# The triangular block inverses of the gated delta rule: their products and subtractions issued on VectorE instead of GpSimd

## The chip, the cores and the metric

The kernel runs on one core of one Trainium2 chip. The metric is the device time of one execution in microseconds; the time quoted for a kernel is the median of its runs. Beside it stands one profiled execution, whose trace gives the start and length of every instruction on TensorE (PE, with its weight loads as PEld), VectorE (DVE), ScalarE (ACT), GpSimd (POOL) and the DMA queues.

## The reference

The program is a two-layer encoder trunk on 512 tokens of 1024 channels in fp32. Layer 0 mixes with attention, layer 1 with a gated DeltaNet of 8 heads of 128 channels; each layer has a half-step SwiGLU feed-forward block before and after its mixer. The change lies in the DeltaNet. There the tokens are cut into chunks, and each chunk of each head needs the inverse of a unit lower triangular matrix:

```
    l_mat = jnp.where(strict, jnp.einsum('bhncd,bhnsd->bhncs', kb, k) * decay, 0.0)
    t_mat = lax.linalg.triangular_solve(l_mat + eye, jnp.broadcast_to(eye, l_mat.shape),
                                        left_side=True, lower=True, unit_diagonal=True)
    u = jnp.einsum('bhncs,bhnsd->bhncd', t_mat, vb)
    def step(state, inp):
        v_new = un - jnp.einsum('bhcd,bhde->bhce', wn, state)
        o = jnp.einsum('bhcd,bhde->bhce', qd, state) + jnp.einsum('bhcs,bhse->bhce', aqk, v_new)
        state = state * cd[..., None, None] + jnp.einsum('bhcd,bhce->bhde', kd, v_new)
```

## The kernel before

All large products are fp32 matmuls made of three products of split operands (`mm3`, lines 179 to 183): weights arrive by SP's DMA queue in panels (`panel`, line 163), ACT rounds a panel to `wh` (line 174) and DVE makes the rest `wl` (line 175). Three panels are held split at a time.

The DeltaNet layer (`odd_mixer`, line 711) takes the eight heads as four pairs, p = 0 to 3. Its projections, gates and output products are one stream, the filler, on TensorE; their results are evicted from two PSUM banks (`mm`) by DVE, as `cx` (line 924, with a depthwise convolution `cy`, lines 927 to 931, behind it) or as `gy` (line 773). Between the filler's steps stand the steps of the delta rule. For one pair of heads they are:

- prep (`gdn_keys`, line 945): the chunk matrices `iu` (line 980) and `du` (line 988) for 128 tokens at a time;
- base (`gdn_base`, line 1016): the inverses of the 32x32 diagonal blocks, 32 blocks to a pair. ACT's DMA queue writes `iu` to DRAM (`iud`, line 1023) and reads the blocks back as `lb`, one block's row per partition (line 1029). Then 31 steps j follow, each a product into `tmp` (line 1035) and a subtraction from `rr` (line 1038) over at most 76 elements per partition, each of these 62 operations needing the one ahead of it. The finished `rr` goes to DRAM by four DMAs on ACT's queue (`rd`, line 1041), and two more bring it back as `r`, one for each head (line 1044);
- scan (`gdn_head`, line 1047): DVE turns `r` into `t` (line 1053); TensorE starts with the products of `t` and `iu` (line 1063, in the trace the rows `pb<-t,iu` with 32*32), doubles the inverses to 64 and 128 rows (lines 1066 to 1083), and then passes over four blocks of 128 tokens, where each block's products wait for DVE's `vb` (lines 1094, 1099) and `state` (lines 1107, 1110). At the end `rs` (line 160, on POOL) scales the output `on` (line 1131), which TensorE turns back (line 784).

The order in which TensorE takes filler and steps is written out: `blend` (line 64) deals the steps by the due times in the table `PLAN`, and a helper keeps the matmuls in that order (line 95). For the other engines a scheduler works out the order of their queues when the program is built, from the order of the program and its own estimate of durations. Each engine takes its queue in order, and an instruction that waits holds all behind it; ACT's DMA issues stand in ACT's queue too. There is one `lb`, one `rr` and one `tmp`, so that a base of one pair begins after the base of the pair ahead.

Of the kernel before, what the change touches and what calls it, by code (L numbers as in the profile page):

```python
# [13 lines left out]
ALU = mybir.AluOpType  # L14
# [87 lines left out]
class Trunk:  # L102
# [913 lines left out]
    def gdn_base(self, pool, G, Ks):  # L1016


        nc = self.nc
        n = BASE  # L1020
        iud = self.dram.tile([2 * HPITCH], F32, tag="iud", name="iud", bufs=2)
        for j, K in enumerate(Ks):
            nc.scalar.dma_start(self.rows_of(iud, j), K["iu"].rearrange("p (t s) -> p t s", s=P))
        lb = pool.tile([P, n, n], F32, tag="lb", name="lb", bufs=1)
        rr = pool.tile([P, n // 4, n], F32, tag="rr", name="rr", bufs=1)
        tmp = pool.tile([P, 9 * n], F32, tag="tmp", name="tmp", bufs=1)
        quarters = [slice(q * 2 * NBLK, (q + 1) * 2 * NBLK) for q in range(4)]
        for s in quarters:
            nc.scalar.dma_start(lb[s], self.blocks_of(iud))
        nc.scalar.copy(out=rr, in_=G["eye"])  # L1030
        for j in range(n - 1):
            m, k = n - 1 - j, j // 4 + 1
            sh = [P, k, m]
            p = tmp[:, :k * m].rearrange("p (a b) -> p a b", b=m)
            nc.gpsimd.tensor_tensor(p, rr[:, :k, j:j + 1].broadcast_to(sh),  # L1035
                                    lb[:, j, j + 1:].rearrange("p (o m) -> p o m", o=1)
                                    .broadcast_to(sh), op=ALU.mult)
            nc.gpsimd.tensor_tensor(rr[:, :k, j + 1:], rr[:, :k, j + 1:], p, op=ALU.subtract)  # L1038
            yield
        for q, s in enumerate(quarters):  # L1040
            nc.scalar.dma_start(self.blocks_of(G["rd"], q, 4), rr[s])
        for j, K in enumerate(Ks):
            K["r"] = pool.tile([P, T], F32, tag="r", name="r", bufs=3)
            nc.scalar.dma_start(K["r"].rearrange("p (t s) -> p t s", s=P), self.rows_of(G["rd"], j))
        yield
# [156 lines left out]
```

## Time and profile before

| what | value |
|---|---|
| median of 3 runs | 2044.92 us (2044.28 to 2045.09) |
| the profiled execution: its own time, its span | 2044.75 us, 2042.9 us |
| TensorE busy | 2011.8 us, 98% of the span |
| DVE, ACT, POOL busy | 1086.6, 747.5, 129.6 us |
| mean granted TensorE clock over the span | 0.994 of full speed |

Busy time of TensorE holds matmuls whose ends are modelled and overlap, so its share says only where it stood idle. In rows of the time line a line in brackets at the end tells how long the engine stood idle before the row and what ended that. A granted clock of 1.00 is TensorE's 2.4 GHz level, and a stretch below it holds time at the 1.2 GHz level.

### The profile page before, as it was taken

Reading aid. Unit: us, or ns where it says so; the run is one execution under the profiler, and the core shown is the slowest. Engines: PE = TensorE matmul, PEld = TensorE weight load, DVE = VectorE, ACT = ScalarE, POOL = GpSimd, SP = SyncE. Lnnn points to the kernel's source line nnn. Section 1 sums busy time; section 2 is a strip of 40 time slices with the busy share of each in tenths; the row PEclk is TensorE's granted clock in tenths of the full one; section 3 lists DMA queues with packets and bytes.
Section 4 is the critical chain, followed back from the end, with each engine's and each line's share of the span. In section 5 each row is a group of like instructions: output and inputs, shape, how many; then the busy total and the mean of one; then the engine's idle time right before and its main releaser. Section 6 shows DMA issues by size and latency. Waiting matters only on the chain.

```text
span 2042.9 us, 24836 instructions
## 1 busy us (share of the span) xinstructions
PE 2011.8 (98%) x9786; PEld 1669.5 (82%) x9786; DVE 1086.6 (53%) x1752; ACT 747.5 (37%) x1359; POOL 129.6 (6%) x294
## 2 busy tenths in 40 slices
PE   8999999999999999999999999998999999999998
PEld 7888888878888888888888888877877788888887
DVE  6442444587676443444544344477677675443543
ACT  5231233454663322323332123354455453322222
POOL 0000000000000000000000000005432400000000
PEclk9999999999999999999999999999999999999999
DMA  4332323222123233232332232334322333323232
GB/s 156 97 99 93 103 93 95 93 70 66 52 75 112 93 94 102 93 102 95 93 98 98 93 103 93 95 114 110 85 75 88 80 99 98 103 83 103 93 98 78
DMA packets 189866, 192.24 MB, mean 94 GB/s; under 512 B 28546, under 2 KB 165044, under 8 KB 189748
## 3 DMA queue, kind: packets, MB, share of 16 engines
q1 hardware_dynamic: 158916, 182.62, 28.5%
q10 hardware_dynamic: 30832, 8.02, 1.7%
q8 instruction: 77, 1.26, 0.3%
q14 instruction: 41, 0.34, 0.1%
HBM read 185.35 MB, written 5.26 MB: 93 GB/s over the span
## 4 chain that ended last, share of the span: by engine, by line
PE 89%; POOL 5%; DMA 2%; DVE 1%; issue 1%; ACT 1%; ACTq 0%; SPq 0%; POOLq 0%
PE mm L181 10%; PE mm L183 10%; PE mm L182 10%; PE pa L181 8%; PE pa L183 8%; PE pa L182 8%; PE pb L181 8%; PE pb L182 8%; PE pb L183 8%; PE mm L96 4%; POOL rr L1038 2%; POOL tmp L1035 2%; PE pb L96 1%; DMA lb<-iud 1%; DMA iud<-iu 1%
## 5 line engine op out<-in xcount | busy, mean ns | idle before, releaser
L175 DVE TENSOR_TENSOR wl<-raw,wh 128x1024 fp32r<-128x1024 f32 (+1 forms) x348 | 413.6, 1189 | 564.5 <-ACT wh L174 563.7
L174 ACT CAST wh<-raw 128x1024 fp32r<-128x1024 f32 (+1 forms) x348 | 355.4, 1021 | 707.5 <-PE pb L182 279.9
L181 PE MATMUL mm<-xnh,wh 128*128 128x512 f32 (+1 forms) x816 | 317.3, 390 | 0.6 <-ACT wh L174 0.6
L183 PE MATMUL mm<-xnh,wl 128*128 128x512 f32 (+1 forms) x816 | 317.8, 390 | 0.0
L182 PE MATMUL mm<-xnl,wh 128*128 128x512 f32 (+1 forms) x816 | 316.8, 389 | 0.0
L181 PEld LDWEIGHTS mm<-xnh,wh 128*128 128x128 f32 x816 | 153.9, 189 | 32.8 <-ACT wh L174 1.2
L183 PEld LDWEIGHTS mm<-xnh,wl 128*128 128x128 f32 x816 | 154.0, 189 | 32.0 <-issue 1.6
L182 PEld LDWEIGHTS mm<-xnl,wh 128*128 128x128 f32 x816 | 154.0, 189 | 30.6 <-issue 0.7
L181 PE MATMUL pa<-xnh,wh 128*128 128x512 f32 x400 | 156.3, 391 | 0.0
L183 PE MATMUL pa<-xnh,wl 128*128 128x512 f32 x400 | 155.8, 390 | 0.0
L183 PE MATMUL pb<-xnh,wl 128*128 128x512 f32 x400 | 155.8, 389 | 0.0
L181 PE MATMUL pb<-xnh,wh 128*128 128x512 f32 x400 | 155.8, 389 | 0.0
L182 PE MATMUL pb<-xnl,wh 128*128 128x512 f32 x400 | 155.8, 389 | 0.0
L182 PE MATMUL pa<-xnl,wh 128*128 128x512 f32 x400 | 155.8, 389 | 0.0
L226 ACT CAST hid<-hd 128x512 fp32r<-128x512 f32 x88 | 54.6, 620 | 209.1 <-DVE hd L398 209.1
L96 PE MATMUL mm<-xnh,wh 128*128 128x512 f32 x256 | 109.7, 428 | 11.5 <-DVE cx L924 11.5
L392 DVE TENSOR_TENSOR gr<-mm,rb 128x512 f32<-128x512 f32 x80 | 55.3, 691 | 94.7 <-PE mm L183 94.5
L182 PE MATMUL pb<-hid,wh 128*128 128x512 f32 x264 | 102.8, 389 | 0.0
L183 PE MATMUL pb<-hid,wl 128*128 128x512 f32 x264 | 102.8, 389 | 0.0
L181 PE MATMUL pa<-hid,wh 128*128 128x512 f32 x264 | 102.8, 389 | 0.0
L183 PE MATMUL pa<-hid,wl 128*128 128x512 f32 x264 | 102.8, 389 | 0.0
L181 PE MATMUL pb<-hid,wh 128*128 128x512 f32 x264 | 102.8, 389 | 0.0
(307 smaller groups left out, 3372.7 us busy)
## 6 DMA issues: line engine op xcount, KB each, us to landing
raw<-in_ffn_w_gate_dram SPq DMA_DIRECT2D x88, 512.0 KB, 3.6
raw<-in_ffn_w_up_dram SPq DMA_DIRECT2D x88, 512.0 KB, 3.5
raw<-in_ffn_w_down_dram SPq DMA_DIRECT2D x88, 512.0 KB, 3.6
raw<-in_gdn_w_in_dram SPq DMA_DIRECT2D x32, 512.0 KB, 3.9
raw<-in_att_w_in_dram SPq DMA_DIRECT2D x24, 512.0 KB, 3.5
raw<-in_gdn_w_out_dram SPq DMA_DIRECT2D x16, 256.0 KB, 2.7
xr<-in_x_dram SPq DMA_DIRECT2D x4, 512.0 KB, 5.4
raw<-in_att_w_out_dram SPq DMA_DIRECT2D x4, 512.0 KB, 3.3
```

What stands on the lines that cost most here:

```text
L96: return self.tc.keep_in_program_order(self.engine.matmul(*args, **kw))
L174: nc.scalar.copy(out=h[:, :n], in_=raw[:, :n])
L175: nc.vector.tensor_tensor(l[:, :n], raw[:, :n], h[:, :n].bitcast(F32), op=ALU.subtract)
L181: self.te.matmul(out, lhsT=lh, rhs=rh, start=start, stop=False)
L182: self.te.matmul(out, lhsT=lh, rhs=rl, start=False, stop=False)
L183: self.te.matmul(out, lhsT=ll, rhs=rh, start=False, stop=stop)
L226: nc.scalar.copy(out=h, in_=src)
L392: nc.vector.tensor_tensor(gr, g[j], self.rb, op=ALU.mult)
L1035: nc.gpsimd.tensor_tensor(p, rr[:, :k, j:j + 1].broadcast_to(sh), lb[:, j, j + 1:].rearrange("p (o m) -> p o m", o=1) .broadcast_to(sh), o ...
L1038: nc.gpsimd.tensor_tensor(rr[:, :k, j + 1:], rr[:, :k, j + 1:], p, op=ALU.subtract)
```

## The change

Both operations of each of the 31 steps are issued on DVE instead of POOL, for all four pairs: 248 instructions. Nothing else in the source differs.

```
             p = tmp[:, :k * m].rearrange("p (a b) -> p a b", b=m)
-            nc.gpsimd.tensor_tensor(p, rr[:, :k, j:j + 1].broadcast_to(sh),
+            nc.vector.tensor_tensor(p, rr[:, :k, j:j + 1].broadcast_to(sh),
                                     lb[:, j, j + 1:].rearrange("p (o m) -> p o m", o=1)
                                     .broadcast_to(sh), op=ALU.mult)
-            nc.gpsimd.tensor_tensor(rr[:, :k, j + 1:], rr[:, :k, j + 1:], p, op=ALU.subtract)
+            nc.vector.tensor_tensor(rr[:, :k, j + 1:], rr[:, :k, j + 1:], p, op=ALU.subtract)
             yield
```

The scheduler lays out the queues of DVE and ACT anew; those of TensorE and SP stay as they are. Three places follow.

On DVE, at the end of the base of pair 0 (the rows from the change's queue set against that of before; + is new). Ahead of this piece, behind the first of two `gy` of line 773, stand the other 35 operations of the base's last 41, one behind the other.

```order
+L1035 TENSOR_TENSOR tmp<-rr,lb 128x24
+L1038 TENSOR_TENSOR rr<-rr,tmp 128x8x3
+L1035 TENSOR_TENSOR tmp<-rr,lb 128x16
+L1038 TENSOR_TENSOR rr<-rr,tmp 128x8x2
+L1035 TENSOR_TENSOR tmp<-rr,lb 128x8
+L1038 TENSOR_TENSOR rr<-rr,tmp 128x8
+L1053 STREAM_TRANSPOSE t<-r 128x512 x2
 L1066 TENSOR_SCALAR pp<-pb 32x128 x4
 L773 TENSOR_TENSOR gy<-mm,rb 128x512
```

The base now ends on DVE directly ahead of the transposes that read its result back, with no other work between. The first 21 operations of this base stand further ahead, singly between other DVE rows.

On ACT, around the DMAs that carry `rr` of pair 0 out and back (lines 1041 and 1044), this was the queue before:

```order
655 L174 CAST wh<-raw 128x1024
656 L932 ACTIVATE c<-cy 128x512
657 L1041 DMA rd<-rr 32x8x32 x4
658 L927 ACTIVATE cy<-cx,conv 128x512
659 L932 ACTIVATE c<-cy 128x512
660 L174 CAST wh<-raw 128x1024
661 L1044 DMA r<-rd 128x4x128 x2
```

So the issue stood ahead of the `cy` that begins the next convolution. In the change the same DMAs of pair 0 stand here on ACT:

```order
666 L970 ACTIVATE kdec<-pa,kd 128x128 x8
667 L774 ACTIVATE gy<-gy 128x512
668 L1041 DMA rd<-rr 32x8x32 x4
669 L1044 DMA r<-rd 128x4x128 x2
670 L1030 COPY rr<-eye 128x256
671 L174 CAST wh<-raw 128x1024
672 L774 ACTIVATE gy<-gy 128x512
```

The issue has moved behind that `cy` and behind the next pair's `kdec` and the first `gy`, and no other work stands between its two halves.

On DVE, where the base of pair 2 begins while pair 1 is in its scan (the change's queue).

```order
1173 L1099 COPY vb<-pb 128x128 x2
1174 L988 SCALAR_TENSOR_TENSOR du_10766<-pb,br,du_10766 128x128 x4
1175 L988 SCALAR_TENSOR_TENSOR du_10804<-pb,br,du_10804 128x128 x4
1176 L1110 COPY state<-pb 128x128 x2
1177 L1035 TENSOR_TENSOR tmp<-rr,lb 128x31
1178 L1038 TENSOR_TENSOR rr<-rr,tmp 128x31
1179 L175 TENSOR_TENSOR wl<-raw,wh 128x512
1180 L1035 TENSOR_TENSOR tmp<-rr,lb 128x30
1181 L785 SCALAR_TENSOR_TENSOR gy<-pa,head,gy 128x512
1182 L1038 TENSOR_TENSOR rr<-rr,tmp 128x30
```

The first product, which waits for the DMAs of line 1029, now stands in the queue of the engine that serves the scan; before, `wl` followed directly on `state`. On POOL the 248 rows are gone, and the operations of line 160 stand behind nothing.

## Rows read from the trace of the kernel before

**Rows 1.** The profile's page, part 1: busy us (share of the span) xinstructions.

```profile
PE 2011.8 (98%) x9786; PEld 1669.5 (82%) x9786; DVE 1086.6 (53%) x1752; ACT 747.5 (37%) x1359; POOL 129.6 (6%) x294
```

**Rows 2.** Time line, TensorE: start us, us, what, count [idle before, releaser].

```profile
1429.06 0.80 PE L96 MATMUL mm<-xnh,wh 128*128 128x512 f32 x1 [6.12 <-DVE cx L924]
...
1438.50 0.89 PE L96 MATMUL pb<-t,iu 32*32 32x32 f32 x32
...
1487.53 0.80 PE L96 MATMUL mm<-xnh,wh 128*128 128x512 f32 x1 [4.83 <-DVE cx L924]
...
1497.87 0.89 PE L96 MATMUL pb<-t,iu 32*32 32x32 f32 x32
...
1563.81 0.89 PE L96 MATMUL pb<-t,iu 32*32 32x32 f32 x32
...
1617.51 1.25 PE L99 MATMUL pa<-ident,on 128*128 128x128 f32 x4 [2.54 <-ACT on L1131]
...
1628.45 0.89 PE L96 MATMUL pb<-t,iu 32*32 32x32 f32 x32
```

**Rows 3.** Time line, POOL and ACT: base of pair 0 begins; ACT issues its result.

```profile
1393.25 0.56 POOL L1035 TENSOR_TENSOR tmp<-rr,lb 128x31 f32<-128x31 f32 x1 [14.79 <-DMA lb<-iud]
...
1424.98 1.82 ACTq L1041 DMA_DIRECT2D rd<-rr  x4
1426.89 0.72 ACT L927 ACTIVATE cy<-cx,conv 128x512 f32<-128x512 f32 x1 [11.63 <-issue]
```

**Rows 4.** Chain that ended last, in order of time: start us, us, what, count.

```profile
1334.73 8.16 PE mm L96 x36
...
1429.06 9.51 PE mm L96 x30
...
1487.53 4.21 PE mm L96 x9
```

**Rows 5.** Four stretches: from:to, us, busy (x) of PE, PEld, DVE, ACT, POOL, clock, DMA, GB/s.

```profile
1393.00:1438.50 45.50, 38.88 (x167) 31.24 (x166) 35.13 (x74) 25.23 (x67) 29.43 (x64) 0.92 0.34 97
1454.90:1497.90 43.00, 38.17 (x200) 31.97 (x198) 25.43 (x56) 22.76 (x74) 25.49 (x64) 0.92 0.20 58
1517.60:1563.80 46.20, 45.75 (x237) 37.47 (x234) 33.92 (x64) 24.82 (x72) 22.76 (x64) 1.00 0.36 106
1592.00:1628.50 36.50, 33.96 (x171) 27.84 (x170) 22.31 (x46) 17.53 (x55) 22.09 (x63) 0.95 0.26 76
```

**Rows 6.** Time line, DVE: small operations, two independent, then two dependent ones.

```profile
1377.13 0.16 DVE L965 TENSOR_TENSOR br<-br,bt 128x4 f32<-128x4 f32 x1
1377.21 0.17 DVE L961 TENSOR_SCALAR sk<-sk 128x4 f32<-128x4 f32 x1
...
1358.52 0.19 DVE L845 SCALAR_TENSOR_TENSOR gyy<-gyy 128x32 f32<-128x32 f32 x1 [3.02 <-ACT gyy L844]
1358.75 0.19 DVE L846 TENSOR_TENSOR gyy<-gyy,nega 128x32 f32<-128x32 f32 x1
```

**Rows 7.** Time line, ACT and DVE: result of base 2 out to DRAM and back.

```profile
1543.24 1.81 ACTq L1041 DMA_DIRECT2D rd<-rr  x4
...
1549.17 0.71 DVE L1053 STREAM_TRANSPOSE t<-r 128x512 f32<-128x512 f32 x1 [0.99 <-DMA r<-rd]
```

**Rows 8.** Time line, DVE and POOL: last DVE row ahead of base 2, and its start.

```profile
1514.34 0.51 DVE L1110 COPY state<-pb 128x128 f32<-128x128 f32 x2 [0.33 <-PE pb L96]
...
1517.66 0.24 POOL L1035 TENSOR_TENSOR tmp<-rr,lb 128x31 f32<-128x31 f32 x1 [13.71 <-DMA lb<-iud]
```

**Rows 9.** Time line, DVE: rows behind which the last base operations stand, pairs 1, 2, 3.

```profile
1494.63 1.23 DVE L175 TENSOR_TENSOR wl<-raw,wh 128x1024 fp32r<-128x1024 f32 x1 [1.65 <-ACT wh L174]
...
1560.19 1.54 DVE L929 SCALAR_TENSOR_TENSOR cy<-cx,conv,cy 128x512 f32<-128x512 f32 x2
...
1625.11 0.68 DVE L227 TENSOR_TENSOR mixl<-gy,mixh 128x512 fp32r<-128x512 f32 x1
```

## The prediction, made before the changed kernel ran

> **What bounds the kernel now.** I read the page first. TensorE is busy 98% of the span [rows 1], so little more than its idle places can be won, and whatever makes it stand is lost. Next I read the waits of TensorE and its time line in the DeltaNet layer. Three stops there matter to this change: 6.12 us before 1429.06, 4.83 us before 1487.53 and 2.54 us before 1617.51 [rows 2]. All three go back to a base on POOL. The reader can follow the first one: the base of pair 0 runs on POOL from 1393.25 and ends where ACT can issue `rd`, at 1424.98; that is 31.7 us for 62 small operations, and ACT, whose queue holds the issue ahead of a `cy`, does nothing else for 11.63 us [rows 3]. DVE then waits for that `cy`, and TensorE for the `cx` behind it. The second stop is the same with pair 1. The third is `rs`, which stands in POOL's queue among the operations of the base of pair 3.
>
> A stop costs more than its idle time. In the chain of work, 36 matmuls without a stop take 8.16 us, 0.227 each; behind the first stop 30 take 9.51 us, 2.7 more than at that rate, and behind the second 9 take 4.21 us, 2.2 more [rows 4]. The granted clock is 0.92 in the stretches that hold these stops and 1.00 in one without [rows 5], so part of them ran at the 1.2 GHz level instead of 2.4. I take 2.2 us for the restart after each stop. The stops that come from POOL are then worth 6.12 + 2.7 = 8.8, 4.83 + 2.2 = 7.0 and 2.54 + 2.2 = 4.7 us, together 20.5 us.
>
> Last I read where TensorE begins with the products of `t`: at 1438.50, 1497.87, 1563.81 and 1628.45 for the four pairs, with no idle time ahead of any [rows 2]. The base is hidden there now. Since the order of TensorE is fixed, these four places decide.
>
> **What one operation costs on DVE.** The trace has none of these on DVE, so I bound them. Two small ones that need nothing of each other start 0.08 us apart; a dependent one starts 0.23 us after the one it needs, at 32 elements [rows 6]. The operations of the long tails have some 50 elements; from 0.16 us at 4 elements to 0.19 at 32 [rows 6] an element costs about 0.001 us, so a dependent step costs 0.25 us. One that stands alone between larger operations finds its input ready: I take 0.15 us, about the middle of 0.08 and 0.23. Below, the end is 0.08 and 0.16 us (the length of the 4-element one); above, POOL's own price, 25.49 us for 64, 0.40 us [rows 5]. I stay by DVE's rows because they are the same engine.
>
> The rows show that a DVE operation may start before its predecessor ends, 0.08 us after a start although each lasts 0.16 [rows 6]. The Trainium skill (VectorE: DVE Perf Modes, "The DRAIN you can't avoid") says that the next operation does not start before the pipe is empty, though it grants an earlier start to some. By that rule each single operation would cost its whole 0.2 us, an estimate from that page's statement, and the sum for pair 0 would be 1 us larger.
>
> **Pair 0.** DVE's work between 1393.0 and 1438.50 is 35.13 us [rows 5]; without two transposes of 0.7 that now come later it is 33.7. The 21 single base operations add 21 x 0.15 = 3.2 us. So the first `gy` is done at 1393.3 + 33.7 + 3.2 = 1430.2; DVE is full throughout and idles nowhere. Then stand 41 base operations in one chain: 41 x 0.25 = 10.3 us, to 1440.5. The way of the result through DRAM comes next: in pair 2 ACT issued at 1543.24 and the first transposed tile was done at 1549.17 + 0.71, 6.6 us later [rows 7]. So `t` is there at 1447.1. TensorE, without its stop of 8.8 us, arrives at 1438.50 - 8.8 = 1429.7 and stands for 17 us. It begins 8.6 us later than now and restarts slowly: **+10.8 us**. ACT's issue, moved behind `kdec` and `gy`, no longer delays anything by itself; what it holds now, `wh` and the second `gy`, waits while TensorE stands anyway.
>
> **Pairs 1 to 3, along the scan.** A base now shares DVE with the scan ahead of it. From rows 5, per stretch, with 62 operations at a mean of 0.2 (12.4 us): pair 1, DVE 25.43 + 12.4 = 37.8 us of work in 43.0 - 7.0 = 36.0 us of TensorE's time, +1.8 us; pair 2, 33.92 + 12.4 = 46.3 us, and here the first operation also waits for its DMAs with `wl` and `vb` queued behind it, from 1514.85 to 1517.66 [rows 8], together 49.1 in 46.2, +2.9 us; pair 3, 22.31 + 12.4 = 34.7 in 36.5 - 4.7 = 31.8, +2.9 us. Sum **+7.6 us**.
>
> **Pairs 1 to 3, at the end of the base.** The last base operations stand behind rows that TensorE itself paces [rows 9], so they cannot end earlier. Pair 1: behind `wl` at 1494.63, 1.2 us, then 4 operations, to 1496.9; plus 6.6 is 1503.5, against 1497.87: a stop of 5.6 + 2.2, in place of one of 7.0: +0.8. Pair 2: between two `cy` that end at 1561.73, so about 1561.1; plus 6.6 against 1563.81: 3.9 + 2.2 = +6.1. Pair 3: behind `mixl` (to 1625.8) and a `wl` of 0.65 us stand 14 operations, 3.5 us, to 1629.9; plus 6.6 against 1628.45: 8.1 + 2.2, less 4.7: +5.6. Sum **+12.5 us**. Each difference is taken within one stretch, so that a shift before it cancels.
>
> **Sum.** 10.8 + 7.6 + 12.5 = 30.9 us on the profiled execution's 2044.75, which is 0.17 below the median: 2075.7, so I say **2076 us**. Costed at nothing: the freed POOL, which is no bound, and `rs`, which becomes free and is in the 4.7. SP's queue is unmoved.
>
> **Bounds.** With the low prices the chains shrink by 41 x 0.09 + 18 x 0.09 = 5.3 us, the single ones of pair 0 by 1.5, the overload by up to 7.6: about 2061. A restart may be worth less after a short stop; that takes 4 more off, 2056 or so. With 0.25 for every operation the overload grows by 3 x 3.1 and pair 0 by 2.1: 2087; with 0.30 it is about 2098.
>
> **Rivals.**
> - *The base simply becomes shorter and its stops go (faster).* On DVE a dependent chain alone is 62 x 0.25 = 15.5 us against 31.7. If it ended that early, nothing would hold ACT or `rs`, and TensorE would gain up to 20.5 us: 2024. For it speaks the price of an operation; against it, the queue: 41 operations behind `gy`, and TensorE at the products of `t` within a microsecond of that `gy`. It decides if `rr` is complete 6.6 us before TensorE asks. The Trainium skill (GPSIMD Engine Reference, 4.1 "Engine selection") has this as its rule, VectorE for elementwise products, GpSimd about twice as slow with two inputs. The trace does not show that factor for an undisturbed operation: 0.24 us on POOL at 31 elements [rows 8] beside 0.23 from start to start on DVE. I give this rival 0.07.
> - *Only pair 0 pays.* If the later bases are hidden after all (DVE finds gaps while TensorE paces it), 10.8 - 7.0 - 4.7 = -0.9 us: 2044, no difference. Chance 0.06.
> - *DVE no better than POOL at these operations.* At 0.40 us each: pair 0 +11.4, overload 3 x 12.4, the later chains 18 x 0.15 = 2.7: 2127, DVE the bound of the whole layer. Chance 0.07; no DVE row in the trace is that dear.
>
> **How the numbers follow.** My forecast has 0.80, almost all of it between 2056 and 2098, which is the range. About 0.2% (4 us) is what a measurement of this kernel can tell from no change. Faster by more than that: 0.07. Within it: 0.06. Slower: 0.80 + 0.07 = 0.87.
>
> **What would show it.** In the changed profile POOL should be nearly empty, DVE's base operations 0.15 to 0.25 us apart, and the waits of TensorE led by DVE's `t` (line 1053) or the DMA behind it, with stops near 17, 6, 4 and 8 us ahead of the four places; the stops ahead of `cx` and `on` should be gone. In the last pairs TensorE should also wait for `vb` or `cx` in small pieces. I am wrong if TensorE begins with `t` of pair 0 without a long stop, or if its lost time sits in the scans rather than at the four places.

## The result and the profile after

| | before | after |
|---|---|---|
| median of 4 runs each, us | 2044.6 (2043.32 to 2045.09) | 2075.23 (2074.30 to 2076.07) |
| ratio, 95% interval | | 1.0148 [1.0135, 1.0161] |
| span of the profiled execution, us | 2042.9 | 2074.3 |

The change makes the kernel 1.5% slower: 2075.2 us against the 2076 of the prediction. Part 1 of the page answers to [rows 1]; of part 2, the slices of TensorE and of its clock:

```profile
PE 2020.4 (97%) x9786; PEld 1676.3 (81%) x9786; DVE 1122.5 (54%) x2000; ACT 748.1 (36%) x1359; POOL 37.3 (2%) x46
...
PE   8999999999999999999999999996989899999998
...
PEclk9999999999999999999999999998989999999999
```

The same row of TensorE on the page of the kernel before:

```profile
PE   8999999999999999999999999998999999999998
```

POOL has lost 92 us of work, DVE has gained 36 for the same 248 operations. By busy time the change is a saving; what it costs stands in three slices of TensorE's row, with 6, 8 and 8 tenths, where the page of the kernel before has 8, 9 and 9.

The next fence is TensorE's time line at the places of [rows 2] (start, us, what, count, idle before and its releaser):

```profile
1446.74 1.63 PE L96 MATMUL pb<-t,iu 32*32 32x32 f32 x32 [17.38 <-DVE t L1053]
...
1455.25 0.59 PE L96 MATMUL pb<-r,pp 32*32 32x32 f32 x16 [1.37 <-ACT r L1083]
1466.55 0.79 PE L96 MATMUL pb<-vb,kdec 128*128 128x128 f32 x4 [0.65 <-DVE vb L1099]
...
1509.92 1.70 PE L96 MATMUL pb<-t,iu 32*32 32x32 f32 x32 [6.68 <-DVE br L962]
...
1582.18 0.87 PE L96 MATMUL pb<-t,iu 32*32 32x32 f32 x16 [3.64 <-DVE t L1053]
1583.43 0.87 PE L96 MATMUL pb<-t,iu 32*32 32x32 f32 x16 [0.38 <-DVE t L1053]
...
1652.37 1.72 PE L96 MATMUL pb<-t,iu 32*32 32x32 f32 x32 [7.81 <-DVE t L1053]
```

The three stops of the kernel before (6.12, 4.83, 2.54 us) are gone, and each of the four places where TensorE asks for `t` now has a stop of its own: 17.4, 6.7, 4.0 and 7.8 us. The third is two rows, 3.64 and 0.38 us. The releaser of the second reads `br`, a small operation of pair 2 that stood on DVE at that moment; the transposes of `t` (line 1053) start at 1509.15 in the same place, so it is the same wait.

Why `t` is late in pair 0 is read from DVE's time line, then ACT's:

```profile
1428.70 0.22 DVE L1038 TENSOR_TENSOR rr<-rr,tmp 128x66 f32<-128x66 f32 x1
1428.84 0.16 DVE L966 TENSOR_TENSOR kd<-br,kdc 128x4 f32<-128x4 f32 x1
...
1429.19 0.68 DVE L773 TENSOR_TENSOR gy<-mm,rb 128x512 f32<-128x512 f32 x1
1429.80 0.21 DVE L1038 TENSOR_TENSOR rr<-rr,tmp 128x63 f32<-128x63 f32 x1
1430.04 0.22 DVE L1035 TENSOR_TENSOR tmp<-rr,lb 128x60 f32<-128x60 f32 x1
1430.30 0.22 DVE L1038 TENSOR_TENSOR rr<-rr,tmp 128x60 f32<-128x60 f32 x1
...
1439.73 0.17 DVE L1038 TENSOR_TENSOR rr<-rr,tmp 128x8 f32<-128x8 f32 x1
1445.97 1.47 DVE L1053 STREAM_TRANSPOSE t<-r 128x512 f32<-128x512 f32 x2 [6.07 <-DMA r<-rd]
```

```profile
1431.04 0.68 ACT L774 ACTIVATE gy<-gy 128x512 f32<-128x512 f32 x1
1439.94 1.82 ACTq L1041 DMA_DIRECT2D rd<-rr  x4
1443.06 0.94 ACTq L1044 DMA_DIRECT2D r<-rd  x2
```

Behind the first `gy` the remaining 41 operations of the base stand in one chain, from 1429.80 to 1439.90: 10.1 us, 0.246 each. An operation that needs the one before it starts 0.25 us after it; one that doesn't (`kd` behind `rr` at 1428.70) starts 0.14 us after it. Then the result goes to DRAM and back, and the first transposed `t` is done at 1446.68. TensorE has nothing else in its order, and stands.

What comes behind a stop is read from the granted clock (from:to, us, busy (x) of PE, PEld, DVE, ACT, POOL, clock, DMA, GB/s):

```profile
1429.70:1446.74 17.04, 0.00 (x1) 0.00 (x1) 9.55 (x44) 2.42 (x8) 0.00 (x0) 0.63 0.26 69
1446.74:1451.00 4.26, 4.26 (x38) 3.62 (x39) 1.87 (x5) 0.16 (x1) 0.00 (x0) 0.50 0.00 0
1509.90:1519.00 9.10, 9.08 (x92) 6.86 (x92) 4.45 (x14) 3.79 (x11) 0.11 (x1) 0.50 0.01 2
1519.00:1522.00 3.00, 3.00 (x28) 2.73 (x28) 2.71 (x6) 0.35 (x1) 0.00 (x0) 0.92 0.29 87
1652.30:1669.00 16.70, 16.63 (x136) 13.33 (x137) 4.88 (x14) 2.37 (x7) 0.00 (x0) 0.50 0.06 18
1669.00:1676.00 7.00, 6.84 (x42) 5.89 (x42) 3.45 (x11) 2.64 (x12) 0.00 (x0) 0.95 0.00 1
```

0.50 is the 1.2 GHz level; the 0.63 of the first row says that the clock fell during the stop. Behind the stop of pair 0 the low level holds for 4.3 us, behind that of pair 1 for 9.1 and behind that of pair 3 for 16.7, with TensorE busy all the time.

Since TensorE's order is the same in both kernels, each of its instructions has a shift, its start after less its start before. The differences between neighbouring shifts say where the 31.4 us came from:

| instruction of TensorE, start before / after | shift | what lies in between | step | predicted |
|---|---|---|---|---|
| `mm` 1433.49 / 1424.67 | -8.82 | old stop of pair 0, restart | -8.8 | -8.8 |
| `t,iu` 1438.50 / 1446.74 | +8.24 | stop ahead of `t`, pair 0 | +17.1 | +17.4 |
| `mm` 1467.16 / 1479.76 | +12.60 | restart (2.0), small waits for `r` and `vb` | +4.4 | +2.2 |
| `mm` 1492.24 / 1497.55 | +5.31 | old stop of pair 1, restart | -7.3 | -7.0 |
| `t,iu` 1497.87 / 1509.92 | +12.05 | stop ahead of `t`, pair 1 | +6.7 | +5.6 |
| `mm` 1523.36 / 1539.63 | +16.27 | restart | +4.2 | +2.2 |
| `mm` 1552.47 / 1567.11 | +14.64 | scan of pair 1 | -1.6 | |
| `t,iu` 1563.81 / 1582.18 | +18.37 | stop ahead of `t`, pair 2 | +3.7 | +3.9 |
| `mm` 1566.58 / 1587.78 | +21.20 | restart | +2.8 | +2.2 |
| `pa` 1622.67 / 1638.69 | +16.02 | old stop of pair 2's `on`, restart | -5.2 | -4.7 |
| `t,iu` 1628.45 / 1652.37 | +23.92 | stop ahead of `t`, pair 3 | +7.9 | +8.1 |
| `mm` 1638.26 / 1669.64 | +31.38 | restart | +7.5 | +2.2 |

The prediction's +7.6 for an overload of DVE along the scans has no row of its own. About one microsecond of it is there, in the scan of pair 0: the first operation of pair 1's base waits on DVE for its DMA, with `vb` queued behind it, and TensorE waits for that `vb` (the 0.65 us at 1466.55 above), where the shift grows by 0.9 us:

```profile
1464.96 0.19 DVE L1035 TENSOR_TENSOR tmp<-rr,lb 128x31 f32<-128x31 f32 x1 [1.54 <-DMA lb<-iud]
```

It is the wait that the prediction had put on pair 2. A wait for `r` in the same scan (1.37 us at 1455.25, 0.5 before) is there as well when no base runs beside it, in the first experiment below. In the scan of pair 1 the shift grows by 0.6 us in small pieces, in those of pairs 2 and 3 not at all.

### The profile page after: what moved, and what is told of

Its sections match the earlier page's. It is cut to its first block, busy times and chain, and to the rows that moved or that the text cites. A ratio compares the mean times of both kernels' runs of the same rounds, so it can differ in the third digit from the quotient of the medians.

```text
span 2074.3 us, 24837 instructions
## 1 busy us (share of the span) xinstructions
PE 2020.4 (97%) x9786; PEld 1676.3 (81%) x9786; DVE 1122.5 (54%) x2000; ACT 748.1 (36%) x1359; POOL 37.3 (2%) x46
## 4 chain that ended last, share of the span: by engine, by line
PE 93%; DVE 2%; DMA 2%; ACT 1%; issue 1%; ACTq 0%; POOL 0%; SPq 0%; POOLq 0%; DVEq 0%
PE mm L181 10%; PE mm L183 10%; PE mm L182 10%; PE pa L181 8%; PE pa L183 8%; PE pa L182 8%; PE pb L181 8%; PE pb L183 8%; PE pb L182 8%; PE mm L96 8%; PE pb L96 3%; PE pb L615 1%; PE pa L99 1%; DVE wl L175 0%; DMA r<-rd 0%
## 5 line engine op out<-in xcount | busy, mean ns | idle before, releaser
L182 PEld LDWEIGHTS mm<-xnl,wh 128*128 128x128 f32 x816 | 153.9, 189 | 30.6 <-issue 0.7
L96 PE MATMUL mm<-xnl,wh 128*128 128x512 f32 x256 | 103.7, 405 | 0.0
L96 PE MATMUL mm<-xnh,wl 128*128 128x512 f32 x256 | 103.6, 405 | 0.0
```

The lines of the kernel that those rows point to most:

```text
L96: return self.tc.keep_in_program_order(self.engine.matmul(*args, **kw))
L182: self.te.matmul(out, lhsT=lh, rhs=rl, start=False, stop=False)
```

## The experiments

The theory is that the price of an operation matters only through the place of the last one: where the last base operation stands in an engine's queue, plus the way through DRAM, against the moment at which TensorE asks for `t`. Its main rival is load: 248 more operations on DVE delay what else DVE does. All experiments were timed beside the kernel before; ratios are to it, with 95% intervals.

**One pair, then the other three.** In both lines of the base, for the first kernel (the second has `if pair`); of the two lines one is shown:

```diff
-            nc.gpsimd.tensor_tensor(p, rr[:, :k, j:j + 1].broadcast_to(sh),
+            (nc.vector if pair == 0 else nc.gpsimd).tensor_tensor(p, rr[:, :k, j:j + 1].broadcast_to(sh),
```

> Only the base of pair 0 is done by VectorE, the bases of pairs 1 to 3 by GpSimd. Theory (the cost is where the last base operation stands in VectorE's queue, place by place): pair 0 has its own terms alone. By the shift of TensorE's instructions between the two profiles it loses 8.8 us of the old stop, gains one of 17.1 and 4.4 us of slow restart: +12.7, so 2057 us (2053 to 2060), with a stop of about 17 us ahead of t of pair 0, and the stops from GpSimd ahead of cx of pair 1 and on of pair 2 as in the kernel before. Rival (VectorE is overloaded by 248 more operations along the scans): pair 0 has no scan beside its base, so its share is small: under 2049.

> Only the bases of pairs 1 to 3 are done by VectorE. Theory: the rest of the shift, 31.4 - 12.7 = +18.7 us, so 2063 us (2059 to 2068), with pair 0's stop of about 6 us ahead of cx as in the kernel before and stops near 7, 4 and 8 us ahead of t of pairs 1 to 3. Rival (overload along the scans): nearly the whole loss is here, 2072 or more, and TensorE waits in many small pieces inside the scans.

Measured: 2057.14 us, 1.0060 [1.0043, 1.0077], and 2066.32 us, 1.0108 [1.0092, 1.0123]. TensorE's time line of the first, and its list of waits of the second:

```profile
1445.21 1.64 PE L96 MATMUL pb<-t,iu 32*32 32x32 f32 x32 [17.43 <-DVE t L1053]
...
1499.54 0.80 PE L96 MATMUL mm<-xnh,wh 128*128 128x512 f32 x1 [5.93 <-DVE cx L924]
```

```profile
PE pb L96 <- DVE t L1053: 20.2, 4, 8.1
PE mm L96 <- DVE cx L924: 7.7, 2, 6.6
```

Each pair brings its own stop and leaves the others' in place. Pair 0 costs 12.8 us by itself, in a stretch without a scan; that excludes load along the scans for it. The three others cost 22.0, three more than expected, with 20.2 us of idle time in four waits for `t`. In the profile of the second the shift also grows by 2.6 us within the scan of pair 0, at waits for `r` and for a `vb` that again stands behind the first base operation: so load has a share, but a small one. The parts add up to 34.8 against 30.6 for the whole, which the intervals allow.

**Asking for `t` later.** The scans begin later in the plan; nothing else changes against the changed kernel (the rest of the table is left out):

```diff
-("scan", 0, 91.5, 1.91)
+("scan", 0, 105.5, 1.2)
-("scan", 1, 138.5, 2)
+("scan", 1, 144.5, 1.7)
-("scan", 2, 202.5, 2.3)
+("scan", 2, 206.5, 2.1)
-("scan", 3, 260.5, 0.95)
+("scan", 3, 267.0, 0.75)
```

> All bases on VectorE as in the change, and the scans of the four pairs begin 14, 6, 4 and 6.5 units later in the plan (a unit is about 1.25 us of TensorE's time there) with a shorter pitch, so that TensorE asks for t later. No operation is added or left out. Theory: the stops ahead of t vanish or shrink to a few us, the stops from GpSimd stay away; ScalarE may now be held by the issue of rd while rr is not ready, which can bring back a stop ahead of cx in pair 0. Between 2024 us (nothing left) and 2045; I expect 2035. Rival (the price or load of the operations on VectorE): the same operations cost the same wherever t is asked for, the time stays within 6 us of 2075.

Measured: 2063.85 us, 1.0094 [1.0079, 1.0109]; neither of the two numbers. 11 us came back, not 40: pair 1's stop vanished and the later two shrank, but pair 0 kept one of 12.5 us. Why stands on DVE and TensorE:

```profile
1432.19 0.86 DVE L980 SCALAR_TENSOR_TENSOR iu<-pa,br,du 128x128 f32<-128x128 f32 x3
1432.97 1.21 DVE L175 TENSOR_TENSOR wl<-raw,wh 128x1024 fp32r<-128x1024 f32 x1
...
1445.56 0.17 DVE L1038 TENSOR_TENSOR rr<-rr,tmp 128x8 f32<-128x8 f32 x1
1453.17 0.71 DVE L1053 STREAM_TRANSPOSE t<-r 128x512 f32<-128x512 f32 x1 [7.43 <-DMA r<-rd]
...
1453.93 0.87 PE L96 MATMUL pb<-t,iu 32*32 32x32 f32 x16 [12.54 <-DVE t L1053]
```

What TensorE does in the time won, the key products of pair 1, sends `iu`, `du` and `wl` into DVE's queue between the operations of the base. The chain now ends at 1445.73, 5.8 us later than in the change, and the way of its result takes 8.2 us instead of 6.8, with ACT's issues of pair 1's `lb` standing among those of `rd` and `r`:

```profile
1445.92 2.08 ACTq L1041 DMA_DIRECT2D rd<-rr  x4
1448.05 1.07 ACTq L1029 DMA_DIRECT2D lb<-iud  x2
1449.41 1.05 ACTq L1044 DMA_DIRECT2D r<-rd  x2
```

TensorE asks 12.0 us later than in the change, the chain ends 5.8 later and the way is 1.4 longer; the stop is shorter by the rest, 4.8. That the place decides fits this; that it can be moved without moving what comes before it was my error.

**The same, with the transfers issued by GpSimd** (`nc.gpsimd.dma_start` on lines 1041 and 1044).

> As e3_late, and the transfers rd<-rr and r<-rd are issued by GpSimd, which is idle there, in place of ScalarE. Theory: whatever e3_late still loses ahead of cx because ScalarE stands at the issue goes: 2 to 10 us less than e3_late, 2024 to 2035. If ScalarE's issue held nobody, the two are the same. If an issue from GpSimd is dear, t comes later and the stops ahead of t return in part, by the same amount for each pair.

Measured: 2071.80 us, 1.0135 [1.0119, 1.0150], 8 us more than the run before it. That is nearest to the last of its three cases, but not by the same amount for each pair: the stops grow by about 2 us in pairs 0 and 2, by some 0.8 in pair 3, and pair 1 has none. From the end of the chain (1445.95) to the first `t` (1455.39 + 0.71) it is 10.2 us:

```profile
1446.28 2.52 POOL L1041 DMA_DIRECT2D rd<-rr  x4 [20.13 <-DVE rr L1038]
1451.99 1.53 POOL L1044 DMA_DIRECT2D r<-rd  x2 [3.19 <-DMA rd<-rr]
```

**More load.** The first 11 products are done twice (the rest of the added call is left out):

```diff
+            if j < 11:
+                nc.vector.tensor_tensor(tmp[:, 4 * n:4 * n + k * m].rearrange("p (a b) -> p a b", b=m),
+                                        rr[:, :k, j:j + 1].broadcast_to(sh),
...
```

> The change, with the product of each of the first 11 steps done twice (the second one into a free part of tmp that nobody reads): 11 more VectorE operations per pair, 44 in all, in the stretches where base operations stand singly among VectorE's other work. Theory (VectorE has slack along the scans, the overload term of the prediction, +7.6 us, is nothing): only pair 0, where VectorE is full, moves, by 11 x 0.15 = 1.7 us; the last operations of the later bases stand behind rows that TensorE paces; 2077 us (2075 to 2079). Rival (overload along the scans is real and has been hidden by other terms): 3 x 11 x 0.15 to 0.25 more, 5 to 8 us, 2082 to 2085.

Measured: 2079.89 us (2077.83 to 2082.34), 1.0173 [1.0157, 1.0188]: between the two, and its interval touches the change's. In the profiled execution, the fastest of its runs, the span is 2076.1, 1.8 us over that of the change; TensorE's waits inside the scans are one of 0.5 and one of 0.2 us, and the stops ahead of `t` of pairs 1 to 3 are 7.5, 6.3 and 8.6 us (6.7, 4.0 and 7.8 in the change). So what the load costs, it costs at three of the four places. Pair 0, where the expectation had its 1.7 us, has a stop of 16.6 us, shorter than the 17.4 of the change: 11 more single operations did not delay it. The size alone would not have told the theories apart.

**A shorter chain.** `for j in range(n - 11)` in place of `range(n - 1)`; the last 10 steps of every inverse are left out.

> The change without the last 10 of the 31 steps (left out: the part of the block inverses that these steps compute, so the output differs): 20 operations fewer in the chain that ends each base. Theory (the chain counts at 0.23 us a step exactly where it ends last): in pair 0 rr is complete 4.6 us earlier, the stop falls from 17.4 to 12.7. In pairs 1 to 3 the stops of 6.7, 4.0 and 7.8 us fall by 1 to 5 us each. On the restart two theories: it hangs on the place (what TensorE does behind the stop), then pair 3 still loses about 7 us behind a stop of some 3 us and the sum is about 2058; or it hangs on the length of the stop, then pair 3's restart falls to 3 or less and the sum is about 2052. Rival (VectorE's load counts, not the chain's end): 80 operations fewer at 0.2 give 16 us spread over the layer with the stops ahead of t as they were.

Measured: 2039.64 us, 0.9975 [0.9966, 0.9985], 36 us less than the change for 80 operations of some 0.2 us. TensorE's waits:

```profile
PE pb L96 <- DVE t L1053: 12.8, 1, 12.8
PE pa L96 <- ACT kdec L970: 2.8, 1, 2.8
```

Pair 0's stop fell to 12.78, as worked out to 0.1 us. The other three did not shrink, they are gone, with their restarts: their last operations now stand ahead of a few large rows of DVE as well. That speaks against load: 42 operations of each base still run on DVE along the scans, and TensorE waits there for no more than 0.5 us at a time. What was expected of the restarts could not be seen, since pair 3 has no stop left behind which to see it.

**What the stops of the kernel before are worth.** Base on GpSimd as before; only the queue that issues `rd` and `r` changes (and GpSimd copies the unit block into `rr`). Shown for GpSimd's queue, with the line for `r` left out; the second kernel has `nc.sync`:

```diff
-        nc.scalar.copy(out=rr, in_=G["eye"])
+        nc.gpsimd.tensor_copy(rr, G["eye"])
-            nc.scalar.dma_start(self.blocks_of(G["rd"], q, 4), rr[s])
+            nc.gpsimd.dma_start(self.blocks_of(G["rd"], q, 4), rr[s])
```

> The kernel before (base on GpSimd), with the copy of the unit block into rr and the transfers rd<-rr and r<-rd issued by GpSimd itself, so that ScalarE holds nothing for rr. This tests the first term of the prediction, that the stops ahead of cx in pairs 0 and 1 come from ScalarE's issue and not from the speed of the base. Theory: both stops (6.1 and 4.8 us) go, 15.8 us with their restarts; but t of pair 0 is then asked for at 1429.7 while rr ends at 1424.3 and the way through memory took 9.4 us when GpSimd issued it: a new stop of about 4 us and its restart; the same for pair 1 about 2 us. Net 2032 to 2042. Rival (the stops come from the slow base itself or from TensorE's order): they stay, 2042 to 2047, or more by what GpSimd's issues cost.

> As e7_pool_queue, but SyncE, whose queue loads the weights, issues the two transfers. The way through memory should be about 6.1 us as from ScalarE, so t of pair 0 is there at about 1430.5: a stop near 1 us. Net 2030 to 2038 if the weights are loaded far enough ahead to bear that SyncE stands at the issue as ScalarE did (11 us in pair 0); if they are not, TensorE waits for wh or wl instead, with stops of 3 to 8 us ahead of mm: 2038 to 2050.

Measured: 2049.28 us, 1.0028 [1.0017, 1.0039], and 2050.82 us, 1.0030 [1.0019, 1.0040]. Both stops ahead of `cx` are gone in both, so their cause was named rightly. But neither kernel is faster. TensorE in the second one:

```profile
1433.85 0.85 PE L96 MATMUL pb<-t,iu 32*32 32x32 f32 x16 [4.41 <-DVE t L1053]
...
1499.40 0.90 PE L99 MATMUL pa<-ident,c 128*128 128x128 f32 x3 [7.17 <-ACT vb L1013]
```

In pair 0 `t` is late next, in pair 1 `rs` (ACT's `vb` stands behind the `on` that needs it). What makes `rs` late differs. In the first kernel it stands in POOL's queue behind the base, which ends at 1487.44, and behind the issue that was put there. In the second the base ends at 1486.86, and POOL then stands 4.25 us at the copy of the unit block, which waits for `rd`; the second `rs` then waits for `a` (line 1127), which DVE has behind a transpose that waits 8.33 us for `r`:

```profile
1491.11 0.40 POOL L1030 COPY rr<-eye 128x256 f32<-128x256 f32 x1 [4.25 <-DMA rd<-rr]
1494.04 0.71 DVE L1053 STREAM_TRANSPOSE t<-r 128x512 f32<-128x512 f32 x1 [8.33 <-DMA r<-rd]
```

So what these two kernels lose there comes in part from what the edit put in.

**Moving the issue within ACT's queue**, behind the next `cy`, and then also the scan of pair 0 by 4 units (left out: the list `cys` of the `cy` instructions, and 57 and 45 empty steps of the plan ahead of the issue in pairs 0 and 1):

```diff
-            nc.scalar.dma_start(self.blocks_of(G["rd"], q, 4), rr[s])
+            with self.tc.issue_after(self.cys[(-1, -2)[pair]].ins) if pair < 2 else nullcontext():
+                nc.scalar.dma_start(self.blocks_of(G["rd"], q, 4), rr[s])
```

> The kernel before (base on GpSimd, transfers issued by ScalarE); only the place of the issue of rd<-rr in ScalarE's queue moves: in pair 0 behind two more cy, in pair 1 behind one more. Theory (the stops ahead of cx come from ScalarE standing at the issue, nothing else): the stops of 6.1 and 4.8 us ahead of cx go, but t of pair 0 is there at about 1424.3 + 0.6 + 7 = 1432 while TensorE asks for it at 1429.7: a stop of 2 to 4 us comes in its place, with a slow restart of 4 to 9 us as in the two runs before. So pair 0 brings -4 to +4 and pair 1 -7 to 0: 2035 to 2048. Rival (the slow base on GpSimd is itself what TensorE waits for): both stops stay, within 2 us of the kernel before.

> As e9_issue_behind_cy, and the scan of pair 0 begins 4 units later in the plan (about 5 us of TensorE's time), with a shorter pitch. Theory: now t of pair 0 is there in time, the stop ahead of it and its slow restart go, and nothing is given back: 6 to 13 us less than the kernel before if pair 1 also gets through (2031 to 2038), 2038 to 2042 if only pair 0 does. Rival (as in e3: what is moved later lets other work in ahead of it and the stop stays): 2044 or more.

Measured: 2044.75 us, 1.0001 [0.9992, 1.0010], and 2044.83 us, 1.0007 [0.9998, 1.0016]. In e9 the first stop becomes one of 5.3 us ahead of `t`; the second stays at 4.83: the issue, one `cy` later, now holds a copy to `on` on ACT for 7.6 us, and DVE stands for that. In e10 `t` of pair 0 stops nobody any more, but `kdec` of pair 1, which ACT now has behind the issue, stops TensorE for 6.2 us, and 8.9 us are lost ahead of the transposes behind `vb` and `rs`. Part of the reason is in the windows of the kernel before and of e10 that hold the base of pair 0 (columns as above):

```profile
1393.00:1425.50 32.50, 29.43 (x137) 23.91 (x135) 25.12 (x51) 14.97 (x39) 26.92 (x62) 1.00 0.33 99
```

```profile
1393.00:1429.50 36.50, 35.46 (x162) 28.90 (x161) 30.85 (x60) 17.68 (x42) 30.22 (x62) 1.00 0.37 107
```

The same 62 operations of POOL are busy for 26.9 us in the kernel before, where DVE is busy 77% of the time because it stands for lack of `cy`, and for 30.2 in e10, where DVE is busy 85%. The base begins 1.1 us later and ends at 1429.3 instead of 1424.9. So with the stop taken away the base itself is later, and with it what waits for it. That DVE's work is what stretches the operations can be read from single rows of the kernel before, two of nearly the same size, the first beside DVE's work, the second while DVE stands:

```profile
1418.20 0.80 POOL L1038 TENSOR_TENSOR rr<-rr,tmp 128x60 f32<-128x60 f32 x1
1419.44 0.29 POOL L1038 TENSOR_TENSOR rr<-rr,tmp 128x54 f32<-128x54 f32 x1
```

Of its 248 operations 43 last over 0.4 us, and DVE is at work beside each of them for at least three quarters of that time; the 74 with nothing of DVE beside them last 0.33 us at most.

The 8.9 us of e10 are not what the next expectation takes them for: its base of pair 1 ends on POOL at 1481.9, and POOL then stands 9.9 us for DVE's `a`, which is behind `wl` and the transposes in DVE's queue.

**A mixture.** Pair 1's base on DVE, the others on GpSimd; issue and scan of pair 0 as in e10, scan of pair 1 as in e3.

> The base of pair 1 alone is done by VectorE, the others by GpSimd; in pair 0 the issue of rd<-rr stands behind two more cy and its scan begins 4 units later, as in e10_issue_and_scan; the scan of pair 1 begins 6 units later with a shorter pitch, as in e3_late. Theory (a stop is won only where what comes next in line is also in time): e10 lost 8.9 us ahead of the transposes of pair 1 because rs stood behind the base in GpSimd's queue; with that base on VectorE rs is free, and t of pair 1 is asked for 7 us later than in the change, so no stop comes there either (e3 had none over 0.2 us at that place). e10's 2044.8 less 8.9 and 2 to 3 of restart: 2032 to 2036, faster than both kernels; with the stop ahead of t of pair 1 back, 2040 to 2046. Rival (the queues are full and every stop only moves): 2043 or more, with a new wait elsewhere.

Measured: 2039.02 us (2036.35 to 2043.03), 0.9974 [0.9965, 0.9983]. That is 3 us short of what the theory gave and faster than both kernels, by 0.26% and 1.7%. TensorE's largest waits:

```profile
PE pa L96 <- ACT kdec L971: 7.6, 3, 4.6
PE pa L99 <- ACT on L1135: 2.5, 1, 2.5
```

None of the four places has a stop ahead of `t` any more, and the long stops ahead of `cx` are gone; of e10's stop for `kdec`, behind the issue of pair 0, 4.6 us are left, and pair 2's `on` still waits for `rs` as before. Both stood in e10 too, so they are not what the theory's number lacks. Nearer to it is the restart that was taken off: the profile has TensorE at the 1.2 GHz level for 6.8 us in the scan of pair 1 all the same, behind waits of 0.5 and 0.8 us only:

```profile
1485.00:1497.80 12.80, 11.52 (x95) 9.24 (x93) 9.47 (x23) 9.09 (x34) 1.77 (x2) 1.00 0.38 106
1497.90:1504.70 6.80, 6.60 (x60) 6.11 (x58) 4.94 (x18) 2.79 (x9) 0.14 (x1) 0.50 0.16 49
```

In the two fastest of the 11 runs, 2036.35 and 2036.56 us, the mean granted clock is 0.999, in the others 0.994 to 0.997. That the low level makes up the missing 3 us is an inference from these numbers; no run tried it.

## Why the prediction came out right, and which terms did not

- *Which wait ends last.* Right: the four stops were put at 17, 6, 4 and 8 us and are 17.4, 6.7, 4.0 and 7.8. In pair 0 every time came out: first `gy` done at 1429.87 (1430.2 predicted), chain 10.1 us (10.3), first `t` used at 1446.74 (1447.1). The chain and the way came out for the reason given, the time of `gy` did not (third point).
- *What the old stops were worth, 20.5 us.* 21.3 by the table. But e7 to e10 show that this sum is no reserve: in each of them one or both of the first two stops went, and as much or more was lost elsewhere, at the next wait in line or, in e7 and e8, also at what the edit put in.
- *The price of an operation, 0.15 and 0.25 us.* The chained one measured 0.246. The single one was too high, and `gy` came out by luck. The prediction had DVE full up to `gy`, 33.7 us of other work and 3.2 for 21 single operations. The profile has it busy for 34.2 of 36.7 us, so that the 21 added well under 1 us, and standing for 2.5, most of it 1.74 us for a `wh`; the waits, put at nothing, filled the place of the price. (The other rows of DVE got a little shorter too, without POOL beside them.)

```profile
1393.00:1429.70 36.70, 36.29 (x167) 29.54 (x165) 34.20 (x93) 24.95 (x66) 2.89 (x2) 1.00 0.34 103
```

- *Overload along the scans, +7.6 us.* Wrong: the table has -1.6 there (the small waits for `on` behind `rs` that the kernel before still had), about 1 us stands at the one wait for `vb`, and e6 shows no long wait. The mean price of 0.2 us was too high: of DVE's 35.9 us more, 10.1 are the chain of pair 0 and 0.7 its single operations, which leaves 25 us for 186, 0.135 each and 8.4 a pair in place of 12.4. With 8.4 the prediction's own sums give 33.8 in 36.0, 45.1 in 46.2 and 30.7 in 31.8 us, no overload in any pair. That rows which may end later (`wl`, `x`) made room besides was not tested.
- *Restart, 2.2 us for each stop, 8.8 us.* Wrong in size: 4.4, 4.2, 2.8 and 7.5, together 18.9 us, some 2.4 of them small waits in the scan of pair 0. I had it from two restarts among full 128x512 products [rows 4]; behind the new stops TensorE does the small products of `t` first, and the 1.2 GHz level holds for up to 16.7 us. For pair 0 the restart alone is 2.0 us, as predicted; it is pair 3's 7.5 that is far off. That the small products are the reason is not shown.
- So the total of 30.9 against 31.4 is partly luck: 9.2 us too much in one term, 10.1 too little in another. Either error alone would still have left the time within the range.

The rival with the base simply becoming shorter had its premise right: a chain of 62 at 0.25 is 15.5 us against 31.7 on POOL. The Trainium skill (GPSIMD Engine Reference, 4.1 "Engine selection") gives a factor of about two for operations with two inputs. The trace agrees for the base as a whole, part of it beside DVE's work. While DVE stood, the last 18 operations took POOL 5.7 us from the first start to the last (1419.07 to 1424.73), against 3.9 for the same 18 on DVE in the change, a factor of 1.4. (The prediction set POOL's 0.24 us of busy time beside DVE's 0.23 from start to start; these are not the same measure.) The rival fell all the same because the operations did not run as a chain until the queue ahead of them was empty.

## What to carry to other kernels

When a dependent chain is moved to an engine that is faster at each step but busy, find where its last step will stand in that engine's queue, add the way to the consumer, and compare this with the moment at which the consumer asks; busy times alone do not tell it. Before counting a stop as gain, look for what is late next, and ask whether the stop was giving someone else time. And give the restart a range of its own: behind the stops of this kernel it cost from 2.0 to 7.5 us, and the same stop with the same work behind it did not always cost the same.

## What the runs showed of the hardware that was not expected

- The 1.2 GHz level behind a stop lasts very differently: 4.3, 9.1 and 16.7 us in one execution. The length of the stop alone doesn't set it. In e3 the stop of pair 3 was 5.3 us instead of 7.8, and the level still held for over 15 us, whereas 17.4 us in pair 0 were followed by 4.3:

```profile
1639.60:1655.00 15.40, 15.40 (x133) 12.43 (x134) 4.73 (x13) 2.47 (x8) 0.00 (x0) 0.50 0.00 2
```

  Nor does the place alone, that is, what TensorE does behind the stop. At pair 3's place the level held for some 17 us in the change, e2 and e5 alike; at pair 1's place, with the same order of work, it held for 9.1 us behind 6.7 us of standing in the change, but for 4.5 behind 7.5 us in e2:

```profile
1500.17:1504.70 4.53, 4.53 (x40) 3.39 (x41) 1.87 (x5) 0.00 (x0) 0.00 (x0) 0.50 0.00 0
```

  Until the clock was back the restart of pair 1 cost 4.0 us in the first and 2.1 in the second. And in e11 the level came without a long stop. What ends it was not tried and stays open.
- The 62 operations of one base took 12% more busy time on POOL (30.2 against 26.9 us) in the run where DVE was the busier beside them; single ones lasted up to 1.2 us beside DVE's work, and at most 0.33 without it.
- Six transfers issued by POOL in e4 took 10.2 us from the end of the chain through DRAM to the first `t`, against 8.2 from ACT in e3, with `lb`'s issues between, and 6.8 from ACT in the change. The four issues of `rd` took 2.52 us on POOL, 2.08 and 1.82 on ACT.
